# A hybrid conv + S5 layer: the loads of the next quarter's u_s moved from the quarter's end to its scan exchange

## The chip, the cores and the metric

The kernel runs on one core of a Trainium2 chip. The metric is the device time of one execution in microseconds. A time is the median of the runs shown; a profile is taken from one more execution, whose own time is given beside its span.

## What is computed

The reference is one layer with two causal token mixers on the same normalised input. The part around the change is the S5 branch:

```
h = RMSNorm(x);  [conv_a, conv_b, z_c, u_s, z_s, g_c, g_s] = split(h @ W_in)
A: GLU -> causal depthwise conv (31) -> LayerNorm -> silu -> * silu(z_c) -> projection
B: u_s in 32 groups of 16 channels; each group drives a 64-dim complex diagonal state
     s_t = Abar s_{t-1} + Bbar u_t,   y_t = Re(C s_t) + D u_t
   y = gelu(y);  y = y * sigmoid(y @ W_glu + b) * silu(z_s) -> projection
out = x + RMSNorm((sigmoid(g_c) * A + sigmoid(g_s) * B) @ W_out)
```

The sequence has 1024 steps, the model 1024 channels, u_s has 512 channels. All of it is float32; a product is made of three passes over operands split into a high and a low part.

## The kernel before

**The order of the work.** Every engine's program is written out in one fixed order. TensorE (PE) computes one product of `seq` after another (`product`, lines 733 to 751: 48 matmuls, or 24 where the contraction has 512 channels). Everything else is put between its matmuls by a small planner (`Clock`, lines 638 to 674): background tasks are generators that yield an estimated VectorE cost and a delay, and `tick` runs those whose estimated time has come, after each group of six matmuls. The tasks are the S5 branch (`s5_chain`, lines 786 to 801), the stores of u_s (`us_rest`, line 893), the depthwise convolution on VectorE (`conv_chain`, line 558; its taps are line 543) and the layer norm. The estimates only fix the order; at run time each engine waits for semaphores.

**u_s.** The projection to u_s is scaled and stored to a scratch in DRAM, one block of 128 channels for each quarter of the groups (`us_out`, lines 190 to 194). `us_in(m)` (lines 196 to 200) reads a block back in another layout, so that 8 time steps and 16 channels lie on the partitions: eight DMAs of 16 partitions each into one tile U.

**A quarter of the S5 branch** (`s5_quarter`, line 370, quarters c = 0 to 3, eight groups each) does, in this order:

- RT from the parameters (VectorE, 397 to 401), transposed on PE into rp (404), copied to R by ScalarE (406);
- O1 (410 to 417); ep = R x U on PE (416), copied to Et by ScalarE (421), exchanged between the partition halves into E2 by two DMAs (423, 424);
- the angles ta, tb, tk (431 to 461) on VectorE; kp on PE (437, 438), copied to kr by ScalarE and VectorE (450, 451), spread into Mt by eight DMAs (458); sine and cosine on ScalarE (463 to 465);
- E2 * Sn, Et * Cs and their sum (467 to 471), the scan Zs (476), eight instructions on VectorE;
- Zs exchanged between the partition halves into Zw by two DMAs (479, 480); Et = Zs * Cs (482), Zw = Zw * Sn (484), Sx (487, 488);
- yp = Mt x U + O1 x Sx on PE (494, 495), gelu on ScalarE into yt (499), yt stored to a scratch (500), and read back as y32 in another layout by eight DMAs (505).

U is thus needed at line 416 and again at line 494.

**The queues.** All DMAs of the kernel are issued by SyncE (SP), one after the other. A DMA that has to wait for its data or for its buffer holds those behind it. Around a quarter SP also carries the weight loads (`wload`, line 698; each goes out when the weight buffer of a product has been split and is free, and feeds the product after the next; `wsplit_h` on ScalarE, line 708, and `wsplit_l` on VectorE, line 716, make the two parts) and the stores of the gates (line 942, `gc` and `zc`).

**The buffers.** The tiles made by `T(...)` (128 x 1024 float32, line 78) share 21 buffers; U, RT, R, Et, Zw, yt, y32 and most others of a quarter are among them. A new tile takes a buffer whose last tile has been used up in program order.

Before the change, `s5_chain` calls `us_in(c)` for c = 1 to 3 at the start of quarter c, after the read of y32 of quarter c - 1; `us_in(0)` is called at line 891.

Of the kernel before, what the change touches and what calls it, by code (L numbers as in the profile page):

```python
# [35 lines left out]
def tile_hybrid_block(  # L36
# [41 lines left out]
    def T(name, dt=F32):  # L78
        return tp.tile([128, 1024], dt, tag="T", name=name)
# [4 lines left out]
    def f32(t):  # L84
        return t.bitcast(F32)
# [110 lines left out]
    def us_in(m):  # L196
        usU[m] = T(f"U{m}")
        src = us_scr[m].rearrange("(g h) (t n) -> t h g n", g=8, t=8)
        for t in range(8):
            nc.sync.dma_start(out=usU[m][16 * (7 - t):16 * (8 - t)].rearrange("p (g n) -> p g n", g=8), in_=src[t])  # L200
# [169 lines left out]
    def s5_quarter(c, P):  # L370
# [15 lines left out]
        def mul(o, x0, x1):  # L386
            V.tensor_tensor(out=o, in0=x0, in1=x1, op=ALU.mult)
# [90 lines left out]
        Zw = T(f"Zw{c}")  # L478
        nc.sync.dma_start(out=Zw[0:64], in_=Zs[64:128])
        nc.sync.dma_start(out=Zw[64:128], in_=Zs[0:64])  # L480
        yield 1.6, 0
        mul(Et, Zs, Cs)
        yield 1.15, 3.0
# [302 lines left out]
    def s5_chain():  # L786
        yield from s5_params(P5)
        for c in range(4):
            while not P5_ready[0]:
                yield 0.0, 0.5  # L790
            if c:
                us_in(c)
            yield from s5_quarter(c, P5)
        yield 0.0, 5.0
        for c in range(4):
            yh[c], yl[c] = T(f"yh{c}", F32R), T(f"yl{c}", F32R)
            A.activation(out=yh[c], in_=y32[c], func=AF.Copy)
            V.tensor_tensor(out=yl[c], in0=y32[c], in1=f32(yh[c]), op=ALU.subtract)
            yield 1.15, 0
        s5_done[0] = True  # L800
        yield 0.0, 0.0
# [15 lines left out]
    for k in range(8):  # L817
        if k == 0:
            us_weights(2)
            load_xt(6)  # L820
            load_xt(7)
            for t in range(3):
                load_x(t)
            clk.add('s5', s5_chain())
# [359 lines left out]
```

## Time and profile before

| | |
|---|---|
| times of the runs, us | 833.16, 830.72, 831.28 |
| median, us | 831.28 |
| the profiled execution, us | 832.25 |
| its span, us | 830.5 |
| granted TensorE clock, mean | 0.996 |
| busy: PE, VectorE, ScalarE, GpSimd | 98%, 75%, 33%, 3% |

The span runs from the first to the last instruction; the rest of the execution's time lies around it. PE is TensorE's matmuls and PEld its weight loads, DVE is VectorE, ACT ScalarE, POOL GpSimd and SPq the queue of SyncE. The granted clock is the share of TensorE's full speed that the chip allowed. Matmuls are pipelined, so two that follow each other overlap in the records.

### The profile page before, as it was taken

How to read it: one execution, taken by the hardware profiler on the slowest of the kernel's cores; microseconds unless marked ns; L12 is line 12 of the kernel's file. 1: busy time of each engine (PE TensorE's matmuls, PEld its weight loads, DVE VectorE, ACT ScalarE, POOL GpSimd, SP SyncE). 2: the span in 40 equal slices, each digit the busy share in tenths (PEclk: the TensorE clock that was granted, in tenths of full speed). 3: DMA queues.
4: the chain of work that ended last, by engine and by line, in shares of the span. 5: the costliest groups of instructions: out<-in, count | busy, mean ns of one | idle time of the engine just before them, and what ended most of it. 6: DMA issues, size and time to landing. Idle time of an engine off the chain costs nothing.

```text
span 830.5 us, 9705 instructions
## 1 busy us (share of the span) xinstructions
PE 815.3 (98%) x3806; PEld 673.7 (81%) x3806; DVE 622.8 (75%) x902; ACT 277.8 (33%) x300; POOL 25.7 (3%) x27
## 2 busy tenths in 40 slices
PE   9999998999999999999999999999999999999996
PEld 6878886888888887888888888888888888888885
DVE  4699895699898989999899889498496644442242
ACT  5862622534425334413321131132166311122121
POOL 3400000000000000000000000000000000000010
PEclk9999999999999999999999999999999999999999
DMA  9713524255434312111112113123252644425152
GB/s 346 279 48 106 167 76 140 78 163 131 127 112 131 98 56 92 60 51 52 39 38 77 64 50 115 51 78 100 102 191 89 228 152 152 152 76 178 51 178 101
DMA packets 40364, 94.97 MB, mean 114 GB/s; under 512 B 8880, under 2 KB 17712, under 8 KB 40320
## 3 DMA queue, kind: packets, MB, share of 16 engines
q1 hardware_dynamic: 40320, 94.36, 34.2%
q8 instruction: 30, 0.49, 0.3%
q14 instruction: 14, 0.11, 0.0%
HBM read 68.00 MB, written 20.97 MB: 107 GB/s over the span
## 4 chain that ended last, share of the span: by engine, by line
PE 55%; DVE 13%; issue 2%; ACT 2%; DMA 2%; SPq 1%; DVEq 0%; POOLq 0%; ACTq 0%
PE pco L741 11%; PE po L1037 10%; PE pgs L741 7%; PE pzc L741 6%; PE pzs L741 5%; PE pca L741 5%; PE pcb L741 5%; PE pso L741 4%; DVE pp L543 3%; PE pgl L741 2%; DVE acc L543 1%; DMA Zw<-Zs 1%; DVE acc L625 1%; PE lnp L582 1%; DVE Zs L476 1%
## 5 line engine op out<-in xcount | busy, mean ns | idle before, releaser
L543 DVE SCALAR_TENSOR_TENSOR pp<-ext,cw,pp 128x512 f32<-128x512 f32 x232 | 166.1, 751 | 5.4 <-ACT pp L534 5.4
L543 DVE SCALAR_TENSOR_TENSOR acc<-ext,hs,acc 128x512 f32<-128x512 f32 x120 | 90.1, 751 | 0.0
L1037 PE MATMUL po<-wox,mgh 128*128 128x512 f32 x192 | 52.3, 389 | 0.0
L519 ACT ACTIVATE ext<-ext 128x1179 f32<-128x1179 f32 x8 | 9.5, 1191 | 100.1 <-DVE ext L518 100.1
L1037 PEld LDWEIGHTS po<-wox,mgh 128*128 128x128 f32 x192 | 36.0, 188 | 7.4
L741 PE MATMUL pgc<-xh,wh_gc 128*128 128x512 f32 x128 | 40.4, 397 | 0.0
L741 PE MATMUL pcb<-xh,wl_cb 128*128 128x512 f32 x128 | 39.6, 391 | 0.5 <-DVE wl_cb L716 0.5
L741 PE MATMUL pca<-xh,wh_ca 128*128 128x512 f32 x128 | 40.0, 394 | 0.0
L1009 DVE TENSOR_TENSOR sgr<-pco,sgr 128x1024 f32<-128x1024 f32 x8 | 9.8, 1225 | 40.1 <-PE pco L741 40.1
L741 PE MATMUL pzc<-xh,wh_zc 128*128 128x512 f32 x128 | 39.8, 392 | 0.0
L741 PE MATMUL pgs<-xh,wh_gs 128*128 128x512 f32 x128 | 39.7, 391 | 0.0
L741 PE MATMUL pca<-xh,wl_ca 128*128 128x512 f32 x128 | 39.5, 390 | 0.1
L741 PE MATMUL pcb<-xh,wh_cb 128*128 128x512 f32 x128 | 39.6, 390 | 0.0
L741 PE MATMUL pco<-cuh,wl_co 128*128 128x512 f32 x128 | 39.5, 390 | 0.0
L741 PE MATMUL pgc<-xh,wl_gc 128*128 128x512 f32 x128 | 39.5, 390 | 0.0
L741 PE MATMUL pgc<-xl,wh_gc 128*128 128x512 f32 x128 | 39.5, 390 | 0.0
L741 PE MATMUL pzc<-xl,wh_zc 128*128 128x512 f32 x128 | 39.5, 389 | 0.0
L741 PE MATMUL pco<-cuh,wh_co 128*128 128x512 f32 x128 | 39.4, 389 | 0.0
L741 PE MATMUL pca<-xl,wh_ca 128*128 128x512 f32 x128 | 39.4, 389 | 0.0
L741 PE MATMUL pgs<-xh,wl_gs 128*128 128x512 f32 x128 | 39.4, 389 | 0.0
L741 PE MATMUL pgs<-xl,wh_gs 128*128 128x512 f32 x128 | 39.4, 389 | 0.0
L741 PE MATMUL pzc<-xh,wl_zc 128*128 128x512 f32 x128 | 39.4, 389 | 0.0
(273 smaller groups left out, 1763.1 us busy)
## 6 DMA issues: line engine op xcount, KB each, us to landing
xt<-in_xt_dram SPq DMA_DIRECT2D x8, 512.0 KB, 6.0
xin<-in_x_dram SPq DMA_DIRECT2D x8, 512.0 KB, 9.8
wr_cb<-in_w_in_dram SPq DMA_DIRECT2D x8, 512.0 KB, 3.6
wr_ca<-in_w_in_dram SPq DMA_DIRECT2D x8, 512.0 KB, 3.3
wr_gc<-in_w_in_dram SPq DMA_DIRECT2D x8, 512.0 KB, 4.1
gc_scratch<-gct SPq DMA_DIRECT2D x8, 512.0 KB, 4.6
wr_zc<-in_w_in_dram SPq DMA_DIRECT2D x8, 512.0 KB, 3.3
zc_scratch<-zct SPq DMA_DIRECT2D x8, 512.0 KB, 2.6
```

What stands on the lines that cost most here:

```text
L476: V.tensor_tensor_scan(out=Zs[:, s], data0=P["r8"][:, g0 + g:g0 + g + 1].to_broadcast([128, 128]), data1=Et[:, s], initial=0.0, op0=ALU.mu ...
L519: A.activation(out=ext[:, :, 0:3, 1:132], in_=ext[:, :, 4:7, 0:131], func=AF.Copy)
L543: V.scalar_tensor_tensor(out=o, in0=src(e, r), scalar=w, in1=o, op0=ALU.mult, op1=ALU.add)
L582: PE.transpose(p[:, t * 128:(t + 1) * 128], acc[c][:, t * 128:(t + 1) * 128], ident)
L625: V.tensor_tensor(out=acc[c], in0=spread[0], in1=acc[c], op=ALU.mult)
L741: PE.matmul(p[:, js(j)], lhsT=lhs[:, ks], rhs=rhs(k, j), start=st, stop=sp_)
L1009: V.tensor_tensor(out=sgt, in0=p, in1=sgt, op=ALU.mult)
L1037: PE.matmul(p[:, js(j)], lhsT=lhs[k][:, s], rhs=rhs[k][:, js(j)], start=st, stop=sp_)
```

## The change

The call of `us_in` for the next quarter goes to the place right after the two Zw exchanges are issued; the call at the start of the quarter goes away.

```diff
@@ s5_quarter
         Zw = T(f"Zw{c}")
         nc.sync.dma_start(out=Zw[0:64], in_=Zs[64:128])
         nc.sync.dma_start(out=Zw[64:128], in_=Zs[0:64])
+        if c < 3:
+            us_in(c + 1)
         yield 1.6, 0
         mul(Et, Zs, Cs)
         yield 1.15, 3.0
@@ s5_chain
             while not P5_ready[0]:
                 yield 0.0, 0.5
-            if c:
-                us_in(c)
             yield from s5_quarter(c, P5)
```

`us_in` has no yield and no cost for the planner, so the instructions of PE, VectorE, ScalarE and GpSimd keep their order. The DMAs stay the same in number and size; 24 of them change their place in SP's queue, and the tile U of quarters 1 to 3 is allocated earlier.

## Rows read from the trace of the kernel before

**Rows 1.** The page, part 1: busy time and share by engine

```profile
PE 815.3 (98%) x3806; PEld 673.7 (81%) x3806; DVE 622.8 (75%) x902; ACT 277.8 (33%) x300; POOL 25.7 (3%) x27
```

**Rows 2.** The chain that ended last: start us, us, what

```profile
218.76 4.17 DMA Zw<-Zs
...
318.50 0.61 DVE wl_glu L716
319.16 15.71 PE pgl L741 x68
```

**Rows 3.** Waits of PE: us in total, times, longest us

```profile
PE ep L416 <- DMA U<-us_scratch: 3.7, 1, 3.7
...
PE ep L416 <- ACT R L406: 0.9, 1, 0.9
```

**Rows 4.** Timeline of PE, quarter 1: start us, us, what [idle before <-releaser]

```profile
134.07 0.61 PE L741 MATMUL pgc<-xh,wl_gc 128*128 128x512 f32 x2
138.37 3.48 PE L416 MATMUL ep<-U,R 128*128 128x128 f32 x16 [3.68 <-DMA U<-us_scratch]
141.60 0.71 PE L741 MATMUL pgc<-xh,wh_gc 128*128 128x512 f32 x2
```

**Rows 5.** Timeline of PE, the same place in quarter 2

```profile
192.31 0.62 PE L741 MATMUL pgc<-xh,wl_gc 128*128 128x512 f32 x2
192.76 1.95 PE L416 MATMUL ep<-U,R 128*128 128x128 f32 x16
194.46 0.71 PE L741 MATMUL pgc<-xh,wh_gc 128*128 128x512 f32 x2
```

**Rows 6.** Windows: us, busy PE PEld DVE ACT POOL, granted clock, DMA share, GB/s

```profile
134.00:138.00 4.00, 0.69 (x4) 0.23 (x2) 3.06 (x4) 0.00 (x0) 0.00 (x0) 1.00 0.74 202
138.00:141.50 3.50, 3.13 (x15) 3.16 (x16) 0.00 (x0) 0.00 (x0) 0.00 (x0) 0.51 0.57 181
```

**Rows 7.** Timeline of SP's queue, quarter 0's scan exchange to quarter 1's loads of U

```profile
106.26 0.59 SPq L480 DMA_DIRECT2D Zw<-Zs  x1
108.09 0.34 SPq L698 DMA_DIRECT2D wr_gc<-in_w_in_dram  x1
...
124.00 0.33 SPq L500 DMA_DIRECT2D ys_scratch<-yt  x1
...
128.29 3.64 SPq L505 DMA_DIRECT2D y<-ys_scratch  x8
131.97 3.74 SPq L200 DMA_DIRECT2D U<-us_scratch  x8
```

**Rows 8.** Timeline of SP's queue behind the scan exchange of quarter 1

```profile
166.86 0.56 SPq L942 DMA_DIRECT2D gc_scratch<-gct  x1
169.31 0.34 SPq L698 DMA_DIRECT2D wr_gc<-in_w_in_dram  x1
```

**Rows 9.** Landing of U's pieces; DMA issues: KB each, median us to landing

```profile
DMA to landing us min/median/max: 2.3/3.0/3.5
...
gc_scratch<-gct SPq DMA_DIRECT2D x8, 512.0 KB, 4.6
```

**Rows 10.** Timeline of VectorE: the wait before kr, and the three before Zw

```profile
147.62 0.28 DVE L451 TENSOR_TENSOR kr<-kp,dmt 16x128 f32<-16x128 f32 x1 [10.47 <-ACT kr L450]
...
170.51 1.23 DVE L387 TENSOR_TENSOR Zw<-Zw,tk 128x1024 f32<-128x1024 f32 x1 [0.57 <-DMA Zw<-Zs]
...
222.95 1.23 DVE L387 TENSOR_TENSOR Zw<-Zw,tk 128x1024 f32<-128x1024 f32 x1 [0.43 <-DMA Zw<-Zs]
...
276.18 1.23 DVE L387 TENSOR_TENSOR Zw<-Zw,tk 128x1024 f32<-128x1024 f32 x1 [1.60 <-DMA Zw<-Zs]
```

**Rows 11.** Timeline of ScalarE: a weight split, R and Et of quarter 1

```profile
127.93 1.05 ACT L708 ACTIVATE wh_gc<-wr_gc 128x1024 fp32r<-128x1024 f32 x1
130.63 1.03 ACT L406 ACTIVATE R<-rp 128x1024 f32<-128x1024 f32 x1 [1.65 <-PE rp L404]
141.88 1.03 ACT L421 ACTIVATE Et<-ep 128x1024 f32<-128x1024 f32 x1 [10.22 <-PE ep L416]
```

## The prediction

> **What bounds the kernel now.** I read the shares of the engines first, then the chain that ended last, then TensorE's own waits, and then the engines' timelines around its one large wait. TensorE (PE) is busy for 98% of the span [rows 1]. The chain that ended last runs on VectorE, ScalarE and the Zw exchanges up to 319.16 us and nearly wholly on PE from there [rows 2]. So both engines carry the time: PE because it is nearly full, VectorE because in the scan quarters PE is only as early as VectorE's results. A microsecond counts where one of the two stands still.
>
> PE's waits name one place. `ep<-U,R` (line 416) waits 3.7 us for a load of U, in one of its four quarters; the next wait of that line is 0.9 us, on ScalarE's R [rows 3]. The timeline places it in quarter 1: a pair of pgc matmuls starts at 134.07, the ep matmuls only at 138.37, and the next pgc at 141.60 [rows 4]. Quarter 2 has the same sequence without a wait: pgc pair at 192.31, ep at 192.76, pgc at 194.46 [rows 5]. Two things are lost in quarter 1. The start is late, and the block is slow: 3.23 us from ep to the next pgc (141.60 - 138.37) against 1.70 (194.46 - 192.76). The windows say why: after the idle stretch the granted clock is 0.51 from 138.0 to 141.5, the level of 1.2 GHz, where it was 1.00 (2.4 GHz) before [rows 6].
>
> Why U is late stands in SP's queue. SP issues the store of yt at 124.00, then holds the eight reads of y32 until that store has landed (128.29), spends 3.64 us on them, and only then reaches the eight loads of U: 131.97, 3.74 us of issue [rows 7]. The last piece leaves the queue at 135.71; a piece lands within 2.3 to 3.5 us of its issue [rows 9], which gives about 138.3, the moment at which ep starts. R, the other operand, is there at 131.66 (130.63 + 1.03) [rows 11].
>
> **The change, part by part.** *The wait in quarter 1.* The loads of U1 now follow the second Zw transfer, whose issue ends at 106.85 (106.26 + 0.59) [rows 7]. At 3.74 us of issue for the eight they are out by 110.6 and landed by 114.1 (+3.5 at most), 20 us ahead of need. R is early too, so ep starts when the queue of PE comes to it: 0.45 us after the pgc pair, as in quarter 2 (192.76 - 192.31), at 134.52. That is 3.85 us earlier than 138.37.
>
> *The slow block.* With PE busy up to ep there is no idle stretch, and in rows 5 the same block at clock 1.00 takes 1.70 us: 1.53 us less than 3.23. Together **5.38 us**, which is also the shift of the next pgc: 141.60 against 134.52 + 1.70 = 136.22. The Trainium skill (TensorE: Matmul & The Clock Gate, Terms) prices such a stretch as the time at the low clock times the lost share of it; the 3.5 us window at 0.51 is about 3.4 us at half clock, hence an estimate of 1.7 us and a sum of 5.55. The two agree within 0.2 us; I keep the rows.
>
> *Does the shift reach the end?* VectorE waits at that place as well: 10.47 us before kr (line 451, at 147.62), which hangs on PE's kp through ScalarE [rows 10]; ScalarE waits 10.22 us before Et, which hangs on ep [rows 11]. When PE comes 5.38 earlier, VectorE still waits 5.09 and ScalarE 4.84. So neither is the next bound there; all three come out of quarter 1 earlier by 5.38, and what follows is the same sequence moved forward. SP is not late either: it is through with its part by 132 instead of 135.71, ahead of the E2 exchange that follows. What is late next is what was late before (R in quarter 3, 0.9 us [rows 3]), moved with the rest.
>
> *Quarters 2 and 3.* In quarter 2 ep did not wait for U [rows 5], and in quarter 3 it waited for R. The earlier loads save nothing there.
>
> *What the moved loads push back.* Three times eight issues (3.74 us of SP) now stand ahead of what followed Zw. In quarter 0 that is a weight load, from 108.09 [rows 7] to 110.6. Weights are loaded two products ahead: this load feeds the ScalarE split that starts at 127.93 [rows 11], so some 17 us cover the 2.5 us of delay and the landing. In quarter 1 a gc store goes from 166.86 to 170.6 and a weight load from 169.31 to about 171.2 [rows 8]; nobody waits for the store, and the weights have a product's time (over 10 us) of cover. In quarter 2 it is the same pair. The yt store of quarter 0 (124.00) comes 13 us after SP is free again, and the other quarters have the same order. At the old place SP simply goes on 3.7 us sooner to a gc store and a weight load. ScalarE, PE and POOL issue the same instructions in the same order. All of this I cost at nothing; the cover would have to shrink by more than 10 us before it cost something.
>
> *Zw itself.* U's pieces now move right behind the two Zw halves, and VectorE's product Zw * Sn waits for Zw: 0.57 us in quarter 1, 0.43 in quarter 2, 1.60 in quarter 3 [rows 10]. The trace has no U behind a Zw, so I bound it. From below: the 512 KB gc store that follows Zw in quarter 1 (166.86 [rows 8, 9]) delays Zw somewhat, and with it gone the waits of quarters 1 and 2 vanish: -1.0 us. From above: Zw lands only after all eight pieces have been issued, +3.74 us in each of quarters 1 and 2; in quarter 0 the 5.09 us left before kr swallow it. That is +7.5 us. I take 0: in quarter 1 that store goes out right behind Zw already and the wait is 0.57, while quarter 3 has the longest wait, 1.60. A follower of the same size does not decide it.
>
> **The sum.** 3.85 + 1.53 = 5.38 us off. The profiled execution took 832.25 us (span 830.5 and 1.75 around it), so it would take 826.9. Its time is 0.97 above the median of the three runs shown, 831.28; against the median I forecast **825.9 us**.
>
> **Rivals.** *Zw comes late.* The mechanism above: place, VectorE's product with Zw in quarters 1 and 2, both before the point at 319.16 where VectorE still holds PE (the chain goes through quarter 2's exchange at 218.76 [rows 2]). At 2.7 us per quarter the gain is gone; at the full 3.74 the kernel takes 833.4 us, 2.1 slower than before. For it: 512 KB more at the same moment. Against it: the store behind Zw in quarter 1, and that U leaves SP after Zw. The Trainium skill (DMA: Bandwidth & Descriptors, Queues, rings and completion order) says that each DMA engine takes descriptors of one ring in order; by that rule U, issued later on the same queue, could hardly push Zw back. Rows 10 agree as far as a store in place of U goes. Chance 0.08, more of it part of the way than the whole.
>
> *SP stands before U.* The loads need a buffer out of the 21 of their pool. If the buffer that U gets at the new place is freed only by the yp matmuls of the same quarter, SP stands from 106.85 until about 124.00, where the store of yp's result goes out, then spends 3.7 us on U, and the weight load of 108.09 leaves at 127.7 and, with a U piece's median of 3.0 us [rows 9], lands at 130.7, 2.8 us after the split at 127.93 wants it. Three quarters cost 8.4 us, less 5.4 gained: **834.3 us**, slower. It decides once SP is held over 13 us. Against it: most tiles of a quarter are short-lived in the code, so that fewer than 21 are in use at a time, and at the old place U's first load went out right behind the y32 reads (131.97) [rows 7]. Chance 0.03.
>
> *The gain is swallowed.* PE waits later for something that does not move with quarter 1. From 141.60 on nothing in the rows points at such a thing: VectorE's and ScalarE's waits keep 5.09 and 4.84 us in hand. If half is lost, the time is 828.6. Chance 0.12.
>
> *It doesn't do what it says.* The wait is not U's but the queue's, or U is held at the new place until late: no change, 831.3. Against it: U's last landing and ep's start agree within 0.1 us. Chance 0.05.
>
> **How the numbers follow.** The forecast case has 0.72. With the Zw bound of -1.0 and 0.6 for the spread of the runs it reaches down to 824.3; upward I take in Zw late by half of what would cancel the gain and half the swallowed gain, 829.2. That leaves out the cases of no gain and of a loss. About 0.3% (2.5 us) is what a measurement of this kernel can tell from no change, so faster means under 828.8. Faster: 0.72, half of the swallowed case and part of the Zw case, 0.82. Same: 0.14, mostly from the no-change, swallowed and Zw cases. Slower: 0.04.
>
> **What would show it.** Right: the loads of U at 106.9 to 110.6 behind Zw in SP's timeline; ep in quarter 1 with no wait on U, its sixteen matmuls in 1.7 us at a granted clock of 1.00 from 134 on; VectorE's wait before kr near 5.1 us; every later landmark, such as the start of pgl at 319.16, earlier by 5.4. Wrong: a wait before Zw * Sn well above 0.57 us in quarter 1 or 0.43 in quarter 2; a weight split on ScalarE that waits for a load; SP standing still before the loads of U; a new wait of PE of over 1 us between 140 and 320.

## The result, and the profile after

The changed kernel takes 828.37 us (median of 7 runs, 827.49 to 828.55), the kernel before, run beside it, 832.45 (7 runs, 830.72 to 835.16). The ratio is 0.9949 with a 95% interval of 0.9934 to 0.9964: about 4.1 us off, against the 5.4 of the forecast. The profiled execution took 828.06 us, with a span of 826.2 where it was 830.5.

The first view is that of PE's waits, which answers to [rows 3].

```profile
PE warm L812 <- DVE warm L809: 1.6, 1, 1.6
PE ep L416 <- ACT R L406: 1.3, 1, 1.3
PE pcb L743 <- DVE wl_cb L718: 0.9, 1, 0.9
...
PE yp L497 <- DVE Sx L490: 0.4, 1, 0.4
```

The wait for U is gone. Two smaller things stand in the list that need an answer: ep's wait for R was 0.9 us and is 1.3, and yp now waits 0.4 us for Sx. The pcb wait (0.9 us where it was 0.5) is near the beginning and is taken up below. (Line numbers between 480 and 789 are two higher than before.)

PE's timeline at the place of [rows 4], and the windows of [rows 6]:

```profile
134.42 0.62 PE L743 MATMUL pgc<-xh,wl_gc 128*128 128x512 f32 x2
134.87 1.95 PE L416 MATMUL ep<-U,R 128*128 128x128 f32 x16
136.57 0.71 PE L743 MATMUL pgc<-xh,wh_gc 128*128 128x512 f32 x2
```

```profile
134.00:138.00 4.00, 4.00 (x27) 3.63 (x26) 3.40 (x4) 1.03 (x1) 0.00 (x0) 1.00 0.52 168
138.00:141.50 3.50, 3.50 (x39) 2.77 (x37) 0.00 (x0) 0.00 (x0) 0.00 (x0) 1.00 0.61 150
```

ep follows the pgc pair by 0.45 us, its block takes 1.70 us (136.57 - 134.87), PE is busy throughout, and the granted clock is 1.00 (2.4 GHz) where it was 0.51.

SP's timeline, for [rows 7 and 8]:

```profile
106.61 0.59 SPq L480 DMA_DIRECT2D Zw<-Zs  x1
107.25 5.19 SPq L200 DMA_DIRECT2D U<-us_scratch  x8
112.55 7.47 SPq L700 DMA_DIRECT2D wr_gc<-in_w_in_dram  x2
...
161.13 0.59 SPq L480 DMA_DIRECT2D Zw<-Zs  x1
161.77 4.52 SPq L200 DMA_DIRECT2D U<-us_scratch  x8
166.38 0.37 SPq L942 DMA_DIRECT2D gc_scratch<-gct  x1
```

The eight loads take 5.19 and 4.52 us of issue, not the 3.74 they took at the old place [rows 7].

VectorE's timeline, for [rows 10], with quarter 0 ahead of them; the bracket is the idle time before the instruction and what ended it:

```profile
111.17 1.23 DVE L387 TENSOR_TENSOR Zw<-Zw,tk 128x1024 f32<-128x1024 f32 x1 [0.78 <-DMA Zw<-Zs]
...
142.57 0.28 DVE L451 TENSOR_TENSOR kr<-kp,dmt 16x128 f32<-16x128 f32 x1 [5.08 <-ACT kr L450]
...
165.80 1.23 DVE L387 TENSOR_TENSOR Zw<-Zw,tk 128x1024 f32<-128x1024 f32 x1 [0.91 <-DMA Zw<-Zs]
...
218.62 1.23 DVE L387 TENSOR_TENSOR Zw<-Zw,tk 128x1024 f32<-128x1024 f32 x1 [0.84 <-DMA Zw<-Zs]
...
271.88 1.22 DVE L387 TENSOR_TENSOR Zw<-Zw,tk 128x1024 f32<-128x1024 f32 x1 [1.62 <-DMA Zw<-Zs]
```

This view shows where the missing microsecond went. In quarter 0 the Zw product has a wait of 0.78 us that it did not have before; the 5.08 us that VectorE stands before kr take it up. Against [rows 10], kr starts 5.05 us earlier (147.62 to 142.57), the Zw product of quarter 1 only 4.71 (170.51 to 165.80), that of quarter 2 4.33 (222.95 to 218.62), that of quarter 3 4.30. The two losses, 0.34 and 0.38 us, go with the growth of the wait in the bracket: 0.57 to 0.91 and 0.43 to 0.84 us. Behind quarter 2 nothing more is lost: the long stretch of pgl on the chain starts at 314.85 where it started at 319.16 [rows 2], 4.31 earlier, and the span is 4.3 shorter:

```profile
314.85 15.71 PE pgl L743 x68
```

The rest, 5.38 - 5.05, is older than the change's first moved DMA: PE's products already run 0.34 us later near the beginning of this execution, long before any DMA that the change moves. PE's timeline there, before and after:

```profile
52.43 0.73 PE L741 MATMUL pcb<-xh,wl_cb 128*128 128x512 f32 x2 [0.51 <-DVE wl_cb L716]
```

```profile
52.77 0.73 PE L743 MATMUL pcb<-xh,wl_cb 128*128 128x512 f32 x2 [0.92 <-DVE wl_cb L718]
```

So the sum closes: 5.38 - 0.34 - 0.34 - 0.38 = 4.32. PE's two new entries are the same losses seen from the other side: yp of quarter 1 waits 0.36 us for the Sx that follows the Zw product, and R of quarter 3, which VectorE starts, comes later against PE by what quarter 2 lost. The experiments agree: with the planner's order as it was, ep's wait for R is 0.9 us in those with no U beside Zw in quarter 2, and 1.3 in those with it.

### The profile page after: what moved, and what is told of

Read it like the earlier page. It is cut to its first block, busy times and chain, and to the rows that moved or that the text cites. A ratio compares the mean times of both kernels' runs of the same rounds, so it can differ in the third digit from the quotient of the medians.

```text
span 826.2 us, 9707 instructions
## 1 busy us (share of the span) xinstructions
PE 813.8 (98%) x3806; PEld 672.6 (81%) x3806; DVE 622.7 (75%) x902; ACT 277.6 (34%) x300; POOL 25.6 (3%) x27
## 4 chain that ended last, share of the span: by engine, by line
PE 76%; DVE 14%; ACT 3%; DMA 3%; issue 2%; POOL 1%; SPq 1%; DVEq 0%; POOLq 0%; ACTq 0%
PE pgs L743 11%; PE pco L743 11%; PE po L1037 10%; PE pcb L743 9%; PE pca L743 8%; PE pzc L743 7%; PE pzs L743 5%; PE pgc L743 5%; PE pso L743 5%; DVE pp L545 3%; PE pgl L743 2%; DVE acc L545 2%; DMA Zw<-Zs 1%; DVE xt L173 1%; PE ep L416 1%
## 5 line engine op out<-in xcount | busy, mean ns | idle before, releaser
L743 PE MATMUL pcb<-xl,wh_cb 128*128 128x512 f32 x128 | 39.4, 389 | 0.0
L743 PE MATMUL pco<-cul,wh_co 128*128 128x512 f32 x128 | 39.4, 389 | 0.0
```

Of the source, the lines that this page charges most:

```text
L743: PE.matmul(p[:, js(j)], lhsT=lhs[:, ks], rhs=rhs(k, j), start=st, stop=sp_)
```

## Experiments

The theory after the result: all of the gain is quarter 1's (3.85 us of waiting and 1.53 of half clock), U needs only to be ahead of the reads of y32 in SP's queue, and its pieces cost some 0.35 us in each of quarters 1 and 2 because they move while Zw is under way and VectorE stands waiting for Zw. The rivals: the gain comes from having all three loads early; the clock plays no part; what SP pushes back costs something. The kernel before, run beside each group, had medians of 833.11 us (first four kernels), 833.28 (next four) and 833.38 (last two).

### Only U of quarter 1 moved

```diff
-        if c < 3:
-            us_in(c + 1)
+        if c == 0:
+            us_in(1)
```

The loads for quarters 2 and 3 are called at the start of the quarter, as before the change.

> Only the loads of U1 move behind Zw (in quarter 0); those of U2 and U3 stay where they were. Theory: the whole gain is quarter 1's (5.4 us: late start 3.85, half clock 1.53), and U behind Zw costs 0.3 us each in quarters 1 and 2, which this kernel does not pay. So 5.0 to 5.4 us under the kernel before, some 0.7 under the changed kernel; the waits before Zw * Sn are about 0.8 in quarter 0, 0.57 in quarter 1, 0.43 in quarter 2. Rival (each of the three moved loads gives something): slower than the changed kernel, a gain of at most two thirds, under 3 us.

827.3 us, ratio 0.9933 (0.992 to 0.9945): 5.8 us below the median of before, a little more than the 5.0 to 5.4 expected. VectorE's timeline, quarters 1 and 2:

```profile
165.51 1.23 DVE L387 TENSOR_TENSOR Zw<-Zw,tk 128x1024 f32<-128x1024 f32 x1 [0.55 <-DMA Zw<-Zs]
...
217.92 1.23 DVE L387 TENSOR_TENSOR Zw<-Zw,tk 128x1024 f32<-128x1024 f32 x1 [0.46 <-DMA Zw<-Zs]
```

The waits are back at 0.55 and 0.46 us. Eight of the 24 moved DMAs bring the whole gain, and without the other sixteen it is larger by about what those waits had grown: 0.75 us in the traces (the table under *Zw itself* below) against 0.34 + 0.38.

### Only U of quarters 2 and 3 moved

```diff
-        if c < 3:
-            us_in(c + 1)
+        if c in (1, 2):
+            us_in(c + 1)
```

The loads for quarter 1 are called at the start of the quarter, as before the change.

> The opposite half: U1 is loaded at the old place, U2 and U3 behind Zw. Theory: quarter 1 keeps its wait of 3.7 us and its stretch at half clock, and the two Zw waits grow by 0.3 to 0.4 us each: 0.5 to 0.8 us slower than the kernel before. Rival (earlier loads help in every quarter): 1 us or more faster.

833.4 us, ratio 1.0006 (0.9997 to 1.0015). PE still waits 3.7 us for U. The wait at the Zw product is that of the changed kernel in quarter 2; in quarter 1 it lies between the two kernels:

```profile
171.28 1.23 DVE L387 TENSOR_TENSOR Zw<-Zw,tk 128x1024 f32<-128x1024 f32 x1 [0.70 <-DMA Zw<-Zs]
...
224.12 1.23 DVE L387 TENSOR_TENSOR Zw<-Zw,tk 128x1024 f32<-128x1024 f32 x1 [0.83 <-DMA Zw<-Zs]
```

These two moves gain nothing and lengthen the two waits by 0.13 and 0.40 us. The total differs from before by less than its interval, so the times alone neither show nor exclude the 0.5 to 0.8 us that were expected; the trace has 0.48 us (the table under *Zw itself* below).

### The loads behind Sx instead of behind Zw

```diff
         V.tensor_tensor(out=v3(Sx)[:, :, 1:128], ..., op=ALU.subtract)
+        if c < 3:
+            us_in(c + 1)
         yield 1.2, 4.5
```

This is against the kernel before, and the call at the start of the quarter goes away here too.

> All three loads move, but to the place behind Sx, some 4 us after the Zw transfers, when Zw has landed. Theory (U's pieces in flight beside Zw make it late): no wait before Zw in quarter 0, 0.57 and 0.43 in quarters 1 and 2 as before the change, quarter 1's wait for U gone; 5.0 to 5.4 us under the kernel before. Rival (Zw is late for another reason, such as the order in SP's queue or the earlier start of the quarter): the waits before Zw stay at 0.8 to 0.9 and the time at that of the changed kernel, 4.2 to 4.4 under the kernel before.

827.46 us, ratio 0.9933 (0.992 to 0.9945). VectorE's timeline, quarters 0 to 2:

```profile
110.81 1.22 DVE L387 TENSOR_TENSOR Zw<-Zw,tk 128x1024 f32<-128x1024 f32 x1
...
165.89 1.23 DVE L387 TENSOR_TENSOR Zw<-Zw,tk 128x1024 f32<-128x1024 f32 x1 [0.57 <-DMA Zw<-Zs]
...
218.31 1.23 DVE L387 TENSOR_TENSOR Zw<-Zw,tk 128x1024 f32<-128x1024 f32 x1 [0.47 <-DMA Zw<-Zs]
```

All 24 loads are moved, but they start 2.2 to 4.2 us behind the second Zw issue instead of 0.6, and the waits are those of before. In quarter 1 a gc store of 512 KB follows Zw here, as in [rows 8]. So not every follower of that size delays Zw; U's pieces do. The traffic differs in kind: in the 5.2 us from Zw's second issue on, the changed kernel's DMA engines move 914 packets for 0.87 MB, 786 of them under 2 KB; this kernel's move 310 for 1.09 MB, 45 of them under 2 KB. That small packets are the reason is only suggested by these rows: the runs vary the place, not the packet, and the store also differs from the loads in its direction and in being one DMA.

### The idle stretch filled, U as late as before

```diff
+        if c == 1:
+            for _ in range(16):
+                PE.matmul(epp[:, 0:512], lhsT=xh[:, 0, 0:128], rhs=xh[:, 0, 0:512], start=True, stop=True)
         pe(lambda g, s: PE.matmul(epp[:, s], lhsT=R[:, s], rhs=U[:, s], ...), 1.8)
```

This is the kernel before, with sixteen matmuls ahead of ep whose result is overwritten.

> The kernel before, with 16 extra 128x512 matmuls on PE ahead of quarter 1's ep (into the same PSUM tile, overwritten by ep), about 3.6 us of work in the 3.85 us in which PE stood still. Theory (the slow block is the half clock after the idle stretch): ep starts as late as before, within 0.3 us of 138.4, but its block takes 1.7 instead of 3.2 us at a granted clock of 1.00; 1.2 to 1.5 us faster than the kernel before. Rival (the block is slow for its operand's sake, pieces of U still landing): the block takes 3.2 us all the same, and the time is unchanged or later.

830.82 us, ratio 0.9976 (0.9967 to 0.9985): 2.3 us below the median of before, more than the 1.2 to 1.5 expected, with more work to do. PE's timeline and the windows:

```profile
135.27 3.79 PE L418 MATMUL ep<-xh 128*128 128x512 f32 x16
138.90 1.95 PE L419 MATMUL ep<-U,R 128*128 128x128 f32 x16
140.61 0.71 PE L744 MATMUL pgc<-xh,wh_gc 128*128 128x512 f32 x2
```

```profile
134.00:138.00 4.00, 4.00 (x20) 3.30 (x19) 3.80 (x5) 0.00 (x0) 0.00 (x0) 1.00 0.64 184
138.00:141.50 3.50, 3.50 (x25) 3.12 (x24) 0.00 (x0) 0.61 (x1) 0.00 (x0) 1.00 0.68 232
```

ep starts even later than in [rows 4], but its block takes 1.71 us instead of 3.23 and the clock stays at 1.00. The clock term can thus be had alone: the block is 1.52 us shorter, where the forecast had 1.53. That ep starts 0.53 us later, when at most 0.3 was expected, is older than the filler: PE is 0.70 us late at the pcb matmul near the beginning (53.13 against 52.43). The whole time is no measure of the clock term, since it holds other differences as well, such as a wait at quarter 3's Zw product of 0.67 us instead of 1.60. That the half clock goes with the idle stretch, and not with ep itself, is shown. The granted clock over a whole execution agrees with it: 0.997 to 0.999 in the eleven runs with the filler, 0.993 to 0.997 in the runs of before beside them.

### The loads just ahead of the reads of y32

```diff
         nc.sync.dma_start(out=ys_scr[c], in_=yt)
+        if c < 3:
+            us_in(c + 1)
         yield 0.0, 5.0
```

This too is against the kernel before, without the call at the start of the quarter.

> The loads of the next U go out right behind the store of yt, ahead of the eight reads of y32 that wait for it, in all three quarters; no U beside Zw. Theory (U was late only because SP held it behind the reads of y32, and a few us earlier is enough): U1 leaves SP from 124.3 to about 128, lands by 131.6, ahead of ep at 134.5; the reads of y32 still begin near 128.3. PE's wait for U is gone, VectorE's waits before the Zw product are 0.57 and 0.43 us in quarters 1 and 2 as before the change, and the time is 5.0 to 5.6 us below before, 0.5 to 1.2 below the changed kernel. Rival (the gain needs the loads 20 us ahead, or the reads of y32 or weight loads behind them become late): PE still waits over 1 us, and under 4 us come off.

827.66 us, ratio 0.9931 (0.9919 to 0.9943). SP's timeline:

```profile
124.69 0.33 SPq L500 DMA_DIRECT2D ys_scratch<-yt  x1
125.07 4.82 SPq L200 DMA_DIRECT2D U<-us_scratch  x8
129.94 3.74 SPq L507 DMA_DIRECT2D y<-ys_scratch  x8
```

PE has no wait for U. Seven microseconds ahead of the old place (131.97 [rows 7]) is enough, the 25 of the change are not needed. The reads of y32 begin at 129.94 and not near 128.3, because U took 4.82 us of issue, and nobody waits for them.

### U loaded twice behind Zw

```diff
         if c < 3:
             us_in(c + 1)
+            keep = usU[c + 1]
+            us_in(c + 1)
+            usU[c + 1] = keep
```

> The changed kernel with each U loaded twice behind the Zw exchange, the second time into a tile that nobody reads: 24 DMAs and 1.5 MB more. Theory (a load behind Zw costs only while Zw is in flight, and what SP pushes back has cover): SP issues 16 pieces in 8 to 10 us, the weight load of quarter 0 leaves near 117 instead of 112.5 and is still 10 us early; VectorE's waits before the Zw product stay at 0.7 to 1.0 us in quarters 1 and 2, since the second eight leave SP after Zw has landed; time within 0.7 us of the changed kernel, 3.5 to 4.9 us below before. Rival 1 (each piece delays Zw): waits of 1.2 us and more, time 0.7 to 2 us above the changed kernel. Rival 2 (SP's pushed back DMAs were not free): a split waits for a weight load or PE for a product, over 2 us above the changed kernel.

827.23 us, ratio 0.993 (0.9917 to 0.9943). SP spends 8.95 us on sixteen loads in quarter 0, the weight load leaves at 116.00, and no split waits for it. The waits at the Zw product are those of the changed kernel, 0.90 and 0.80 us in quarters 1 and 2: the second eight do not lengthen them, as the theory has it. But the time is 6.1 us below before, where at most 4.9 was expected, and the span is 1.3 us shorter than the changed kernel's (824.9 against 826.2), which none of the theories had. Of that, 0.3 us is older than the first moved DMA (the pcb matmul at 52.46 instead of 52.77). ScalarE's timeline shows another difference, first the changed kernel, then this one:

```profile
142.44 1.00 ACT L941 ACTIVATE gct<-pgc 128x1024 f32<-128x1024 f32 x1
146.05 1.28 ACT L463 ACT_TABLE_LOAD   x1 [2.61 <-DVE ta L461]
147.34 1.15 ACT L463 ACTIVATE tk<-ta,cst 128x1024 f32<-128x1024 f32 x1
```

```profile
142.16 1.00 ACT L944 ACTIVATE gct<-pgc 128x1024 f32<-128x1024 f32 x1
143.17 1.28 ACT L463 ACT_TABLE_LOAD   x1
145.72 1.15 ACT L463 ACTIVATE tk<-ta,cst 128x1024 f32<-128x1024 f32 x1 [1.26 <-DVE ta L461]
```

In quarter 1 of the changed kernel the table load for sine waits 2.61 us for ta, which only the activation behind it reads, and then costs 1.28 us on the path. Here it runs while ScalarE has nothing else to do. VectorE's next weight split starts 1.56 us earlier (150.19 against 151.75), 1.25 of it beyond the older difference. The view of that line shows what held the load, again the changed kernel first:

```profile
L463 ACTq EVENT_SEMAPHORE  x3: 17/4372/4806, 146.0 to 249.0; - x3
```

```profile
L463 ACTq EVENT_SEMAPHORE  x2: 4371/4588/4804, 193.4 to 247.6; - x2
```

In the changed kernel a separate wait instruction (17 ns, at 146.0) stands in ScalarE's queue just ahead of the load of quarter 1; here quarter 1 has none, and the load runs at once. No engine reads the second U. That the extra tiles change which buffers the later ones get, and that this takes the wait away, I argue from the code; it was not tried by itself.

### The Zw product later in the planner's order

Two kernels with the loads behind Sx and another delay ahead of the product, 4.0 in one and 5.0 in the other:

```diff
         mul(Et, Zs, Cs)
-        yield 1.15, 3.0
+        yield 1.15, 5.0
         mul(Zw, Zw, Sn)
```

> As the version with the loads behind the Sx instruction, and the planner's delay ahead of the Zw product is 4.0 instead of 3.0, so that VectorE does up to one more piece of the convolution while Zw is under way. Theory (VectorE's standing at the Zw product holds PE's end, about 0.57 + 0.47 + 1.6 us of it in quarters 1 to 3): waits of quarters 1 and 2 vanish, that of quarter 3 falls under 1.0, and the time is 1 to 2.5 us below the version with the old delay, 6.5 to 8 us below before. Rival (the standing in quarter 3 is not on the path, or the later Sx makes PE wait at yp or moves the order elsewhere): no change against the old delay, or slower.

> The same with a delay of 5.0. Theory: all three waits before the Zw product vanish (1.6 us in quarter 3 too), 2 to 2.7 us below the version with the old delay, 7 to 8 us below before. Rival: Sx comes so late that PE waits for it at yp (0.4 us now), and the time is equal to that with 4.0 or above it.

With 4.0: 828.71 us, ratio 0.9943 (0.9929 to 0.9956), 1.2 above the old delay and 4.6 below before, where 6.5 to 8 was expected. With 5.0: 824.31 us, ratio 0.9891 (0.9878 to 0.9904), 9.0 below before, where 7 to 8 was expected. In both, VectorE's waits before the product are gone in all quarters, so my price for those waits (2.6 us in all) fails in the one and is too low in the other. The windows (columns as in [rows 6]) say more, first for 4.0, then for 5.0:

```profile
195.00:250.00 55.00, 53.98 (x288) 45.07 (x287) 51.22 (x69) 20.55 (x20) 0.95 (x1) 1.00 0.44 111
250.00:300.00 50.00, 49.56 (x240) 41.37 (x239) 44.15 (x68) 23.60 (x25) 0.00 (x0) 1.00 0.33 94
```

```profile
195.00:250.00 55.00, 55.00 (x303) 46.69 (x302) 49.01 (x66) 21.90 (x22) 0.95 (x1) 1.00 0.43 119
250.00:300.00 50.00, 50.00 (x261) 41.88 (x260) 45.24 (x63) 23.42 (x24) 0.00 (x0) 1.00 0.37 103
```

With 5.0 PE has not a gap from 85 to 340 us; with 4.0 it still waits for R in quarter 3 (1.0 us), and further on 1.0 us for the statistics of the layer norm. The delay reorders everything behind it, and which later piece decides between the two was not separated. One candidate is the table load of the section above: in quarter 1 it waits 1.66 us for ta with 4.0 and not at all with 5.0.

### The delay without the move, and with it

The same delay of 5.0, once in the kernel before and once in the changed kernel.

> The kernel before (loads of U at the start of each quarter) with the delay of 5.0 ahead of the Zw product, as in the fastest version so far. Theory (the late U and the planner's delay are two separate losses): PE still waits 3 to 4 us for U in quarter 1 and has a stretch at half clock; 4 to 5.5 us above the version that has both the delay and the moved loads, so 3.5 to 5 us below before. Rival (with the later product ep of quarter 1 comes late enough that U has landed): no wait of PE for U, and the time within 0.7 us of the version with both.

> The changed kernel (loads of U right behind the Zw exchange) with the delay of 5.0. Theory (U's pieces beside Zw cost something only because VectorE stood waiting for Zw): with more pieces of the convolution ahead of the product the waits before it are 0 in quarters 1 to 3, and the time is within 0.5 us of the version with the loads behind Sx and the same delay, 8 to 9.5 us below before. Rival (the pieces beside Zw cost the path something besides that wait): 0.7 us or more above it.

In the kernel before: 833.25 us, ratio 0.9998 (0.9987 to 1.0009), no gain where 3.5 to 5 us was expected. In the changed kernel: 823.93 us, ratio 0.9892 (0.9878 to 0.9906), 9.4 us off and the fastest of all. PE's timeline at ep of quarters 1 and 3 in the first, then in the second:

```profile
139.80 2.02 PE L416 MATMUL ep<-U,R 128*128 128x128 f32 x16 [1.69 <-DMA U<-us_scratch]
...
253.12 3.75 PE L416 MATMUL ep<-U,R 128*128 128x128 f32 x16 [3.47 <-DMA U<-us_scratch]
256.53 1.20 PE L741 MATMUL pzc<-xh,wh_zc 128*128 128x512 f32 x2
```

```profile
137.42 1.95 PE L416 MATMUL ep<-U,R 128*128 128x128 f32 x16
...
247.00 1.95 PE L416 MATMUL ep<-U,R 128*128 128x128 f32 x16
```

And the window behind the second wait in the first of the two:

```profile
253.00:257.00 4.00, 3.88 (x17) 3.91 (x18) 2.83 (x3) 0.08 (x1) 0.00 (x0) 0.50 0.63 206
```

With the loads at their old place the wait for U moves: 1.69 us in quarter 1, and now 3.47 us in quarter 3, with the granted clock at 0.50 behind it. I had expected 3 to 4 us in quarter 1 alone. Behind the 1.69 us of quarter 1 the block still takes 1.78 us (139.80 to the next pgc at 141.58), behind the 3.47 us 3.41 (256.53 - 253.12). The two places hold the difference between these kernels' traces, all but 0.53 us that is older (ep of quarter 0): ep of quarter 1 is 2.38 us apart, ep of quarter 2 2.49, ep of quarter 3 6.12, and behind its slow stretch kr of quarter 3 is 8.84 apart (263.53 and 254.69); the spans differ by 8.8 (830.7 and 821.9). So the two edits are not a sum: the delay is worth nothing while U is late, and the move is worth 9.3 us under the delay (833.25 - 823.93) against 4.1 without it. With the delay, the place right behind Zw costs nothing either (823.93 against 824.31 behind Sx): VectorE has work until Zw has landed, and its trace has no wait before the product.

## Why the prediction was right, and what it mis-sized

The mechanism was right, and the time lies in the range.

*The wait in quarter 1* held: ep 0.45 us behind the pgc pair as forecast, no wait for U. U was out later than forecast (112.44 instead of 110.6), and that was of no account.

*The slow block* held: 1.70 us at a granted clock of 1.00, and the filled stretch showed the clock's part alone, with 1.52 us against the forecast's 1.53. The Trainium skill's estimate in the prediction (TensorE: Matmul & The Clock Gate, Terms), 1.7 us, is 0.2 above that measurement.

*Does the shift reach the end?* The waits left in hand were as forecast: VectorE 5.08 us before kr (5.09), ScalarE 4.85 before Et (4.84):

```profile
136.86 1.03 ACT L421 ACTIVATE Et<-ep 128x1024 f32<-128x1024 f32 x1 [4.85 <-PE ep L416]
```

Nothing of the 5.05 us at kr was swallowed on the way except at Zw.

*What the moved loads push back* cost nothing that shows, even doubled: no split and no product waits for it. The weight load of quarter 0 left at 112.55 us instead of the forecast 110.6, and its split at 128.28 did not wait. SP did not stand before U, which answers that rival. (Its price used a U piece's 3.0 us of landing for a weight load; the page of before has 4.1 for wr_gc, so the rival was priced too low.)

*Zw itself* is the step that failed, as the term that was mis-sized: I took 0, and it is 0.34 us in quarter 1 and 0.38 in quarter 2, 0.72 of the 1.07 us by which the shift of pgl fell short (5.38 against 4.31); the other 0.34 was there before the first moved DMA. Taking that start off in every trace gives, in us:

| kernel | pcb matmul near 52 us | first matmul of pgl | pgl against before, counted from pcb |
|---|---|---|---|
| before | 52.43 | 312.15 | |
| changed | 52.77 | 307.85 | 4.64 earlier |
| only U of quarter 1 | 52.83 | 307.16 | 5.39 earlier |
| only U of quarters 2 and 3 | 53.16 | 313.36 | 0.48 later |
| behind Sx | 53.21 | 307.52 | 5.41 earlier |
| ahead of the reads of y32 | 53.08 | 307.40 | 5.40 earlier |

In the three kernels that load U of quarter 1 early and move no U beside Zw in quarters 1 and 2, the 5.38 of the forecast comes out within 0.03 us; in the changed kernel 0.74 of it is lost. One of the signs that I had named for being wrong, a wait before Zw * Sn above 0.57 us in quarter 1 or 0.43 in quarter 2, did show. The direction is that of the rival in which Zw comes late, at a tenth of its full price. My reason for 0 was that a store of the same 512 KB follows Zw already; the kernel with the loads behind Sx has that store again, and 0.57 us again, so the size alone does not tell what a follower does. I also took the issue of U at 3.74 us wherever it stands, and it took 4.52 to 5.19. The Trainium skill's sentence that I leaned on for this rival (DMA: Bandwidth & Descriptors, Queues, rings and completion order), one ring taken in order, goes on to say that a later descriptor may finish its write before an earlier one. The rows do not bear out the use I made of the first half: Zw's median to landing went from 3.4 to 3.9 us with U behind it. The order of single writes no run here shows.

*The base.* I set the 5.38 against the median of three runs, 831.28. The seven runs of before have 832.45, the later ones 833.1 to 833.4. With the loss at Zw and this base the forecast would have been 832.45 - 4.66 = 827.8. Both misses lie on the same side; the range still holds the result because its upper end had left room for half a loss.

## What to carry to other kernels

A load that waits only because it stands behind a DMA that waits for data should go ahead of that DMA in the queue; here 7 us further ahead were enough, and the best place is one at which no engine stands waiting for a transfer just issued. An idle stretch of TensorE is priced with the slow stretch behind it, where the rows show one: here 1.5 us on top of 3.9, and next to nothing behind a wait of 1.69 us. And a second edit should be measured with the first in place: a later scan product gained nothing alone and 3.2 (loads behind Sx) to 4.4 us (loads behind Zw) once U was early.

## What was not expected of the hardware

- Eight 64 KB loads of U take 3.74 to 3.92 us of issue on SP behind the reads of y32 in the kernel before, and 4.52 to 5.19 us right behind the two 256 KB transfers of Zw in the changed one; the longest single issue went from 431 to 1076 ns. What sets it is not shown: behind a 512 KB store of yt it was 4.82 us.
- A transfer issued later on the same queue can lengthen the landing of the earlier one: VectorE's wait for Zw grew by 0.13 to 0.41 us with 512 KB in pieces of 64 KB behind it, and by nothing that could be seen with a 512 KB store in one piece.
- An activation table load can stand behind a wait that belongs to the activation behind it: 1.3 us on the path in quarter 1 of the changed kernel, gone in the kernel that loads U twice, where no wait instruction stands ahead of the load. Why it is not there was not tried.
